# Reordering the first two column blocks of a gated up-projection on one core

## The chip, the cores and the metric

The kernel runs on one core of a Trainium2 chip. The number that counts is the device time of one execution, in microseconds (us). An execution runs five engines side by side, each with an instruction queue of its own that is worked off in order: PE (TensorE, matrix products; its weight loads are shown apart as PEld), DVE (VectorE), ACT (ScalarE), POOL (GpSimd) and SP (SyncE, which here issues the transfers). Engines wait for each other by semaphores.

## The reference

One layer of a transformer: 1024 positions, model width 1024, everything in float32.

```
h  = RMSNorm(x);  P = h @ W_in
A  = multi-head latent attention (MLA), 8 heads        -> 512 columns
Bm = chunked attention ("ca"), 8 heads                 -> 512 columns
x += concat(RMSNorm(A), RMSNorm(Bm)) @ W_out
u  = causal depthwise conv3( RMSNorm(x) @ W_up ) + conv_b      # W_up: 1024 x 5632, two halves g and v
x += ( silu(g) * v ) @ W_down                                  # W_down: 2816 x 1024
```

## The kernel before

**Products.** TensorE multiplies rounded operands. A float32 matrix is split into a rounded high part (a copy, on ACT) and a low part (value minus high part, a subtraction on DVE or POOL), and `mm3` makes one product of three matmuls: high by high, low by high, high by low (lines 137, 138 and 139 of the helper, so all products of the kernel carry these three lines). Here the high part is ready first and the low part one or two instructions later.

**Out-projection.** It goes by 8 tiles of 128 positions, in `order = [0, 4, 1, 5, 2, 3, 6, 7]`. The half that belongs to "ca" has been accumulated and added to x earlier; the last stage adds the half that belongs to "mla". Step i of that stage, for tile t = order[i], multiplies (`out_proj`), transposes the normalised rows of the tile before (`trans2`, line 1223), adds the product to x on DVE (`out_add`, line 1126), takes the norm (`norm2`), turns the tile before into its share of the operands of the next stage (`quarters`), and normalises its own rows on DVE (`scale2`, tile h, line 1173).

**Up-projection.** It goes by 22 column blocks j. The activations are cut into four quarters B11, B21, B22 and so on by positions and model width, the weights of a block into A11, A12, A21, A22, and a block is made of seven products instead of eight: A11, S2, S1, S3, A12, A22, S4 (12 matmuls each), with sums of weights (S1 to S4, on POOL) on one side and sums of activations (T1 to T4, held with high and low parts in tiles hq) on the other. `quarters` makes T1, T2, T3 of a tile with t >= 4 on DVE out of PSUM, their high parts on ACT and their low parts on POOL (`put(..., G)`, line 1209), and subtracts for T4 on POOL (line 1248). `make_w` and `put_w` split the weights (tiles wop, lines 1320 and 1325). `combine(j, n)` adds a finished product to the sums of its block: U2, U4, U3 and, in place, in the two double-bank PSUM tiles "ps" of the block (line 1404); one such tile is the "v" half of a block (S3 in one bank, A22 in the other), the second the "g" half (A12 and S4). Single banks are "pb". `conv` runs the three taps (ACT line 1349, DVE lines 1352 and 1353), `glu` the activation, and `pair` makes the four additions "as" on every odd block (DVE lines 1387 to 1390) for the down-projection.

**What sets the order.** The program is written out by hand; the order of the text is the order on each engine, there is no scheduler. `slot(d, fn)` puts a function d products later: `step()` counts the products of the loop over j, so `slot(1, ...)` runs after the next product has been issued. Block 0 and the first two products of block 1 are written out ahead of that loop, mixed with what belongs to the last tile (tile 7: `scale2(7)`, `trans2(7)`, its T1, T2, T3, B22). `make_early` splits the weights A11 and A12 of block 0 (tiles woph on ACT, wopl on POOL, lines 1259 and 1260); at the end of step i = 4 their transfer is issued.

A wait on PSUM is kept for a whole tile: a matmul into one bank of a "ps" tile waits for what reads or writes the other bank of it, where that stands ahead of it in the program.

Of the kernel before, what the change touches and what calls it, by code (L numbers as in the profile page):

```python
# [14 lines left out]
ALU = mybir.AluOpType  # L15
# [24 lines left out]
W0_LO_V = (1, "A11"), (1, "A12"), (0, "S4")  # L40
W_LO_V = "S2", "S1", "A22"
WO_AT = 146, 154, 162, 170
# [36 lines left out]
def trunk(ctx, tc, a, out):  # L79
# [4 lines left out]
    V, A, G, T = nc.vector, nc.scalar, nc.gpsimd, nc.tensor  # L84
# [17 lines left out]
    def blk(dt=F32, n="b"):  # L102
        return pool.tile([128, 1024], dt, name=name(n), tag="blk", bufs=NBLK)
# [4 lines left out]
    def small(tag, dt, n, bufs):  # L108
        return pool.tile([128, 512], dt, name=name(n), tag=tag, bufs=bufs)

    def p2(dt, n):
        return small("p2", dt, n, 10)
# [4 lines left out]
    def ps():  # L117
        return pp[0].tile([128, 1024], F32, name=name("ps"), tag="d", bufs=nb[0])

    def bank():  # L120
        return pp[0].tile([128, 512], F32, name=name("pb"), tag="b", bufs=nb[1])
# [11 lines left out]
    def f(ap):  # L133
        return ap.bitcast(F32)

    def mm3(o, lh, ll, rh, rl, start, stop):
        T.matmul(o, lh, rh, start=start, stop=False)  # L137
        T.matmul(o, lh, rl, start=False, stop=False)  # L138
        T.matmul(o, ll, rh, start=False, stop=stop)  # L139
# [366 lines left out]
    ca = {}  # L506
# [284 lines left out]
    slot = -8  # L791
# [240 lines left out]
    order = [0, 4, 1, 5, 2, 3, 6, 7]  # L1032
# [2 lines left out]

    def out_part(kind, t, c, j):
        if j == 0:
            if kind == "ca":
                part[kind, t, c] = bank()
            elif c == 0:  # L1040
                p = ps()
                part[kind, t, 0], part[kind, t, 1] = p[:, 0:512], p[:, 512:1024]
        wh, wl_ = wo[(4 if kind == "ca" else 0) + j]
        hi, lo = O[kind, j]
        w = slice(512 * c, 512 * c + 512)
        mm3(part[kind, t, c], hi[:, t * 128:(t + 1) * 128], lo[:, t * 128:(t + 1) * 128], wh[:, w], wl_[:, w], j == 0,
            j == 3)
# [29 lines left out]
    for s in range(NS + LAG):  # L1077
        if s < NS:
            n, i, pc_ = flat[s]
# [37 lines left out]
    def rows(d, t):  # L1117
        return d[t * 128:(t + 1) * 128]
# [82 lines left out]
    def put(name_, o, src, lo_eng, now=True):  # L1201

        s3 = src.rearrange("p (k s) -> p k s", k=4)
        for hi, ks in Q[name_].cols(0, o):
            A.activation(hi, s3[:, ks], AF.Copy)

        def lo_part():
            for (hi, ks), (lo, _) in zip(Q[name_].cols(0, o), Q[name_].cols(1, o)):
                lo_eng.tensor_tensor(lo, s3[:, ks], f(hi), op=ALU.subtract)  # L1209

        if now:
            lo_part()
        return lo_part
# [12 lines left out]
    def quarters(t, p):  # L1226
        u, o = t % 4, (t % 4) * 128
        if t == 3:
            F.append(blk(F32, "F"))
        F0 = F[u]  # L1230
        if t < 4:
            for i, n in enumerate(("B11", "B21")):
                lo = put(n, o, p[i], V, False)
                A.activation(F0[:, 512 * i:512 * i + 512], p[i], AF.Copy)
                lo()
            return
        T3, T1, T2 = [p2(F32, "T") for _ in range(3)]
        lo = put("B22", o, p[1], V, False)
        V.tensor_tensor(T1, p[0], F0[:, 0:512], op=ALU.subtract)
        A.activation(T3, p[0], AF.Copy)  # L1240
        lo()
        V.tensor_tensor(T2, p[1], T1, op=ALU.subtract)
        V.tensor_tensor(T3, p[1], T3, op=ALU.subtract)
        put("T1", o, T1, G)
        put("T2", o, T2, G)
        put("T3", o, T3, G)
        T4f[u] = T2
        G.tensor_tensor(T2, T2, F0[:, 512:1024], op=ALU.subtract)

    Q["B11"], Q["B21"] = Quarter(True), Quarter(True)  # L1250
# [11 lines left out]

    new_psum("psc", 2, 4)
    for i, t in enumerate(order):
        if i == 7:
            make_early()
        p = out_proj("mla", t, i == 7)
        q = trans2(order[i - 1]) if i else None
        out_add("mla", t, 0, p[0])
        out_add("mla", t, 1, p[1])  # L1270
        norm2(t)
        if i:
            quarters(order[i - 1], q)
        if i < 7:
            scale2(t)
            nc.sync.dma_start(rows(x2d, t), x2[t])
        if i < 6:
            load_x2(order[i + 2], x2d)
        if i == 4:
            for k in range(2):  # L1280
                nc.sync.dma_start(wst[k].rearrange("p (k c) -> p k c", k=4),
                                  dap(w_up, 4 * k * 128 * 2 * DFF, [[2 * DFF, 128], [128 * 2 * DFF, 4], [1, 128]]))

    ad = nc.dram_tensor("act_scratch", (7, NFF // 2, 128, 512), F32, kind="Internal").ap()
    wbig = big(F32, "wstage")
    NAMES = ("A11", "S2", "S1", "S3", "A12", "A22", "S4")
    HALF = {"A11": "B11", "A12": "B21", "S4": "B22", "A22": "T4", "S1": "T1", "S2": "T2", "S3": "T3"}

# [10 lines left out]
    def make_w(j, n, lag=1):  # L1299

        st = wbig[:, 2048 * (j % 2):2048 * (j % 2) + 2048]
        A11, A12, A21, A22 = [st[:, 512 * i:512 * i + 512] for i in range(4)]
        if n == "S2":
            S1 = wtmp["S1"] = p2(F32, "S1")
            S2 = wtmp["S2"] = p2(F32, "S2")
            G.tensor_tensor(S1, A21, A22, op=ALU.add)
            G.tensor_tensor(S2, S1, A11, op=ALU.subtract)
        if n == "S3":
            wtmp["S3"] = p2(F32, "S3")
            G.tensor_tensor(wtmp["S3"], A11, A21, op=ALU.subtract)  # L1310
        if n == "S4":
            wtmp["S4"] = p2(F32, "S4")
            G.tensor_tensor(wtmp["S4"], A12, wtmp["S2"], op=ALU.subtract)
        put_w(j, n, wtmp[n] if n in wtmp else {"A11": A11, "A12": A12, "A22": A22}[n], lag)
# [14 lines left out]
    pair = {}  # L1329
# [32 lines left out]
    def slot(d, fn):  # L1362

        if d:
            todo.setdefault(now[0] + d, []).append(fn)
        else:
            fn()
# [6 lines left out]
    def glu(j, g, v):  # L1374
        A.activation(g, g, AF.Silu)
        act[j] = v
        q = j // 2

        def mul():
            (V if j == NFF - 1 else G).tensor_tensor(v, g, v, op=ALU.mult)  # L1380
            slot(STORE, lambda: nc.sync.dma_start(ad[4 * (j % 2), q], v[:, 0:512]))

        def pair():
            e = act.pop(j - 1)
            A11, A21, A12, A22 = e[:, 0:512], e[:, 512:1024], v[:, 0:512], v[:, 512:1024]
            s = [p2(F32, "as") for _ in range(4)]
            V.tensor_tensor(s[0], A21, A22, op=ALU.add)  # L1387
            V.tensor_tensor(s[1], s[0], A11, op=ALU.subtract)  # L1388
            V.tensor_tensor(s[2], A11, A21, op=ALU.subtract)  # L1389
            V.tensor_tensor(s[3], A12, s[1], op=ALU.subtract)  # L1390

            def store():
                nc.sync.dma_start(ad[5, q], A22)
                for i, d in enumerate((2, 1, 3, 6)):
                    nc.sync.dma_start(ad[d, q], s[i])

            slot(STORE, store)

        slot(1, mul)
        if j % 2:  # L1400
            slot(2, pair)

    def add(d, x_, y, op=ALU.add):
        V.tensor_tensor(d, x_, y, op=op)  # L1404
# [54 lines left out]
    W21, W22 = wbig[:, 1024:1536], wbig[:, 1536:2048]  # L1459
    scale2(7)  # L1460
    make_w(1, "A11", 0)
    make_w(1, "A12", 0)
    S1 = p2(F32, "S1")
    V.tensor_tensor(S1, W21, W22, op=ALU.add)
    q = trans2(7)
# [3 lines left out]
    T3, T1, T2 = [p2(F32, "T") for _ in range(3)]  # L1469
    F0 = F[3]  # L1470
    V.tensor_tensor(T1, q[0], F0[:, 0:512], op=ALU.subtract)
    A.activation(T3, q[0], AF.Copy)  # L1472
    combine(0, "A11")
    V.tensor_tensor(T2, q[1], T1, op=ALU.subtract)
    V.tensor_tensor(T3, q[1], T3, op=ALU.subtract)
    put("T1", 384, T1, V)
    put_w(0, "S1", S1)
    product(0, "S1")
    lo = put("B22", 384, q[1], V, False)
    put("T2", 384, T2, V)  # L1480
    V.tensor_tensor(W21, wst[0], W21, op=ALU.subtract)
    V.tensor_tensor(wst[0], S1, wst[0], op=ALU.subtract)
# [2 lines left out]
    G.tensor_tensor(T2, T2, F0[:, 512:1024], op=ALU.subtract)  # L1485
    T4f[3] = T2
    product(0, "S2")
    lo()
    V.tensor_tensor(wst[1], wst[1], wst[0], op=ALU.subtract)
    put_w(0, "S4", wst[1])  # L1490
    product(0, "S4")
    put_w(0, "S3", W21)
    combine(0, "A12")
    product(0, "S3")
    Q["T4"] = Quarter(True)
    for u in range(4):
# [114 lines left out]
    for j in range(1, NFF):  # L1611
        for i, n in enumerate(NAMES):
            if j > 1 or n not in ("A11", "A12"):
                product(j, n)
            if j == NFF - 1:
                if i == 1:
                    ring += [big(F32R, "aring"), big(F32R, "wring")]
                if i < AHEAD:
                    load_step(*dsteps[i])
                if i >= 4:  # L1620
                    split_step(i - 4, *dsteps[i - 4])
            step()
            if i == 1 and j + 2 < NFF:
                load_up(j + 2)
            if j > 1 or n not in ("A11", "A12"):
                slot(1, lambda j=j, n=n: combine(j, n))
            if j + 1 < NFF:
                make_w(j + 1, n)
    xb += [big(F32, "x2b") for _ in range(2)]
    for n, (i, q) in enumerate(dsteps):  # L1630
# [8 lines left out]
        if n in X2_AT:  # L1639
            t = X2_AT.index(n)  # L1640
# [30 lines left out]
```

## Time and profile before

| | |
|---|---|
| time, median of 3 runs | 1291.77 us (1290.53 to 1293.58) |
| profiled execution: its own time | 1291.74 us |
| profiled execution: span in the trace | 1289.7 us |
| granted clock of TensorE, mean (1.0 is 2.4 GHz) | 0.991 |
| PE busy | 1230.5 us, 95% of the span |
| DVE busy | 968.5 us, 75% |
| POOL busy | 724.8 us, 56% |
| ACT busy | 634.0 us, 49% |

The span runs from the first to the last recorded instruction; the time of the execution is 2.0 us longer. All instants below are in us from the start of the span. The up-projection of the blocks spoken of here lies between 630 and 710.

### The profile page before, as it was taken

How to read it: one execution, taken by the hardware profiler on the slowest of the kernel's cores; microseconds unless marked ns; L12 is line 12 of the kernel's file. 1: busy time of each engine (PE TensorE's matmuls, PEld its weight loads, DVE VectorE, ACT ScalarE, POOL GpSimd, SP SyncE). 2: the span in 40 equal slices, each digit the busy share in tenths (PEclk: the TensorE clock that was granted, in tenths of full speed). 3: DMA queues.
4: the chain of work that ended last, by engine and by line, in shares of the span. 5: the costliest groups of instructions: out<-in, count | busy, mean ns of one | idle time of the engine just before them, and what ended most of it. 6: DMA issues, size and time to landing. Idle time of an engine off the chain costs nothing.

```text
span 1289.7 us, 17903 instructions
## 1 busy us (share of the span) xinstructions
PE 1230.5 (95%) x5920; PEld 1012.2 (78%) x5920; DVE 968.5 (75%) x1663; ACT 634.0 (49%) x1306; POOL 724.8 (56%) x753
## 2 busy tenths in 40 slices
PE   7999998999998988999979999999999999999998
PEld 7888886777786766788757888888888888878887
DVE  4786757888989898465886766776766777788983
ACT  6681344667776766404553443343343344434442
POOL 3578743667676777203675766766766750435630
PEclk9999999999999999999998999999999999999999
DMA  5101222111111121263513233233233236933253
GB/s 205 48 27 49 59 68 71 26 42 43 30 28 40 42 63 50 98 229 138 173 58 113 68 99 122 93 112 123 72 92 123 90 131 229 392 109 102 73 188 131
DMA packets 101315, 130.57 MB, mean 101 GB/s; under 512 B 11783, under 2 KB 60519, under 8 KB 101223
## 3 DMA queue, kind: packets, MB, share of 16 engines
q1 hardware_dynamic: 99431, 125.17, 29.8%
q0 software_dynamic: 1792, 4.26, 1.7%
q8 instruction: 47, 0.77, 0.2%
q14 instruction: 45, 0.37, 0.1%
HBM read 93.27 MB, written 31.81 MB: 97 GB/s over the span
## 4 chain that ended last, share of the span: by engine, by line
PE 50%; DVE 8%; issue 2%; ACT 1%; DMA 1%; POOL 0%; DVEq 0%; ACTq 0%; SPq 0%
PE pb L138 10%; PE pb L137 10%; PE pb L139 10%; PE ps L137 6%; PE ps L139 6%; PE ps L138 5%; DVE as L1388 1%; DVE ps L1404 1%; DVE as L1387 1%; DVE x2b L1404 1%; DVE as L1389 1%; DVE wop L1325 1%; DVE as L1390 0%; PE pb L1223 0%; DVE h L1173 0%
## 5 line engine op out<-in xcount | busy, mean ns | idle before, releaser
L921 POOL TENSOR_TENSOR plo<-misc,phi 128x512 fp32r<-128x512 f32 (+2 forms) x144 | 149.3, 1044 | 72.9 <-ACT phi L906 59.1
L137 PE MATMUL ps<-hq,wop 128*128 128x512 f32 x344 | 136.7, 397 | 9.9 <-DVE ps L1404 7.3
L1349 ACT ACTIVATE u<-ps,cols 128x1024 f32<-128x1024 f32 x44 | 53.1, 1207 | 187.0 <-DVE ps L1404 187.0
L139 PE MATMUL ps<-hq,wop 128*128 128x512 f32 x344 | 135.2, 393 | 1.2 <-DVE wop L1325 1.2
L138 PE MATMUL ps<-hq,wop 128*128 128x512 f32 x344 | 135.4, 393 | 0.2 <-DVE hq L1209 0.2
L903 ACT ACTIVATE misc<-pb 128x512 f32<-128x512 f32 (+1 forms) x192 | 89.3, 465 | 82.6 <-POOL plo L921 26.7
L1325 POOL TENSOR_TENSOR wop<-S,wop 128x512 fp32r<-128x512 f32 x42 | 62.7, 1492 | 108.0 <-ACT wop L1320 108.0
L138 PE MATMUL pb<-wring,aring 128*128 128x512 f32 x308 | 120.2, 390 | 1.9 <-DVE wring L1578 1.9
L137 PE MATMUL pb<-wring,aring 128*128 128x512 f32 x308 | 120.1, 390 | 0.1
L139 PE MATMUL pb<-wring,aring 128*128 128x512 f32 x308 | 120.0, 390 | 0.0
L137 PE MATMUL pb<-hq,wop 128*128 128x512 f32 x264 | 103.1, 391 | 2.0 <-ACT T L1472 1.0
L139 PE MATMUL pb<-hq,wop 128*128 128x512 f32 x264 | 103.0, 390 | 0.0
L138 PE MATMUL pb<-hq,wop 128*128 128x512 f32 x264 | 102.9, 390 | 0.0
L1575 DVE TENSOR_TENSOR aring<-ast,aring 128x512 fp32r<-128x512 f32 x77 | 71.2, 924 | 36.6 <-ACT aring L1574 36.6
L1574 ACT ACTIVATE aring<-ast 128x512 fp32r<-128x512 f32 x77 | 48.5, 630 | 95.1 <-PE pb L138 74.9
L137 PEld LDWEIGHTS ps<-hq,wop 128*128 128x128 f32 x344 | 65.3, 190 | 28.2 <-DVE ps L1404 13.0
L906 ACT ACTIVATE phi<-pb 128x512 fp32r<-128x512 f32 (+3 forms) x185 | 87.0, 470 | 0.0
L139 PEld LDWEIGHTS ps<-hq,wop 128*128 128x128 f32 x344 | 65.3, 190 | 15.3 <-DVE wop L1325 1.5
L138 PEld LDWEIGHTS ps<-hq,wop 128*128 128x128 f32 x344 | 65.4, 190 | 13.9 <-DVE hq L1209 0.7
L137 PE MATMUL pb<-wh,hTh 128*128 128x512 f32 x192 | 76.2, 397 | 0.0
L138 PE MATMUL pb<-wl,hTh 128*128 128x512 f32 x192 | 76.0, 396 | 0.1
L139 PE MATMUL pb<-wh,hTl 128*128 128x512 f32 x192 | 75.4, 393 | 0.0
(341 smaller groups left out, 3601.2 us busy)
## 6 DMA issues: line engine op xcount, KB each, us to landing
wstage<-in_w_up_dram SPq DMA_DIRECT2D x43, 512.0 KB
ast<-act_scratch SPq DMA_DIRECT2D x77, 256.0 KB
act_scratch<-as SPq DMA_DIRECT2D x44, 256.0 KB
wd<-in_w_down_dram SPq DMA_DIRECT2D x44, 256.0 KB
act_scratch<-u SPq DMA_DIRECT2D x33, 256.0 KB
x<-in_x_dram SPq DMA_DIRECT2D x16, 512.0 KB
ws<-in_w_in_dram SPq DMA_DIRECT2D x32, 256.0 KB
x_scratch<-x SPq DMA_DIRECT2D x14, 512.0 KB
```

Of the source, the lines that this page charges most:

```text
L137: T.matmul(o, lh, rh, start=start, stop=False)
L138: T.matmul(o, lh, rl, start=False, stop=False)
L139: T.matmul(o, ll, rh, start=False, stop=stop)
L903: A.activation(p32[:, w], o[:, w], AF.Exp, scale=sc_)
L906: A.activation(phi[:, w], o[:, w], AF.Exp, scale=sc_)
L921: e.tensor_tensor(plo[:, w], p32[:, w], f(phi[:, w]), op=ALU.subtract)
L1325: (V if n in W_LO_V or (j, n) in W0_LO_V else G).tensor_tensor(lo, s, f(hi), op=ALU.subtract)
L1349: A.activation(u, U, AF.Identity, scale=convw(2, c), bias=convb(c))
L1387: V.tensor_tensor(s[0], A21, A22, op=ALU.add)
L1404: V.tensor_tensor(d, x_, y, op=op)
L1574: A.activation(ah, s, AF.Copy)
L1575: V.tensor_tensor(al, s, f(ah), op=ALU.subtract)
```

## The change

Nothing is computed otherwise; what changes is the order of the program and, for a few operations, the engine or the kind of PSUM tile:

- (a) `out_part`: the first MLA tile (t == order[0]) is accumulated in two single banks rather than in a double-bank tile.
- (b) `quarters` of tile 6 (called in step i = 7): the low parts of its T1 and T2 are put off, and made on DVE instead of POOL, after `make_w(1, "A11", 0)`; its subtraction for T4 on POOL is put off to the same place.
- (c) `make_early` is called in step 6 rather than in step 7.
- (d) the four "as" additions of blocks 0 and 1 stand at slot 4 rather than at slot 2.
- (e) `combine(0, "A11")`, a copy on ACT, stands before `trans2(7)`.
- (f) the low part of the B22 quarter of tile 7 is made right after its high part, and both ahead of T1's parts.
- (g) `combine(0, "A12")` stands after `product(0, "S2")`, two products earlier.
- (h) `combine(1, "S3")` stands at slot 2 rather than at slot 1, that is after product A22 of block 1 has been issued.

```diff
     def out_part(kind, t, c, j):
         if j == 0:
-            if kind == "ca":
+            if kind == "ca" or t == order[0]:
                 part[kind, t, c] = bank()
...
-        put("T1", o, T1, G)
-        put("T2", o, T2, G)
+        late = [put("T1", o, T1, V if t == 6 else G, t != 6), put("T2", o, T2, V if t == 6 else G, t != 6)]
         put("T3", o, T3, G)
         T4f[u] = T2
+        if t == 6:
+            return late + [lambda: G.tensor_tensor(T2, T2, F0[:, 512:1024], op=ALU.subtract)]
         G.tensor_tensor(T2, T2, F0[:, 512:1024], op=ALU.subtract)
...
     for i, t in enumerate(order):
-        if i == 7:
+        if i == 6:
             make_early()
...
         if i:
-            quarters(order[i - 1], q)
+            late = quarters(order[i - 1], q)
...
         slot(1, mul)
         if j % 2:
-            slot(2, pair)
+            slot(2 if j > 1 else 4, pair)
...
     scale2(7)
     make_w(1, "A11", 0)
+    for fn in late:
+        fn()
     make_w(1, "A12", 0)
+    combine(0, "A11")
...
     A.activation(T3, q[0], AF.Copy)
-    combine(0, "A11")
     V.tensor_tensor(T2, q[1], T1, op=ALU.subtract)
     V.tensor_tensor(T3, q[1], T3, op=ALU.subtract)
+    put("B22", 384, q[1], V)
     put("T1", 384, T1, V)
     put_w(0, "S1", S1)
     product(0, "S1")
-    lo = put("B22", 384, q[1], V, False)
     put("T2", 384, T2, V)
...
     product(0, "S2")
-    lo()
+    combine(0, "A12")
     V.tensor_tensor(wst[1], wst[1], wst[0], op=ALU.subtract)
     put_w(0, "S4", wst[1])
     product(0, "S4")
     put_w(0, "S3", W21)
-    combine(0, "A12")
     product(0, "S3")
...
             if j > 1 or n not in ("A11", "A12"):
-                slot(1, lambda j=j, n=n: combine(j, n))
+                slot(2 if (j, n) == (1, "S3") else 1, lambda j=j, n=n: combine(j, n))
```

Line numbers behind the first hunks move by one, and by three or four from the sixth hunk on (1404 becomes 1405, 1387 becomes 1388, 1325 becomes 1326, 1471 becomes 1475).

On PE, where product A22 of block 1 begins and S4 follows (ps_7324 and ps_7325 are the "v" tile of block 1, ps_7367 and ps_7368 its "g" tile), the rows of before are:

```order
L139 MATMUL ps_7324<-hq_6562,wop_7263 128x512
L137 MATMUL ps_7324<-hq_7215,wop_7266 128x512 [waits DVE_49]
L138 MATMUL ps_7324<-hq_7215,wop_7266 128x512
...
L139 MATMUL ps_7324<-hq_7215,wop_7266 128x512
L137 MATMUL ps_7367<-hq_6549,wop_7289 128x512 [waits Activation_49]
```

and of the change, on the same engine at the same place:

```order
L139 MATMUL ps_7325<-hq_6562,wop_7264 128x512
L137 MATMUL ps_7325<-hq_7216,wop_7267 128x512
L138 MATMUL ps_7325<-hq_7216,wop_7267 128x512
...
L139 MATMUL ps_7325<-hq_7216,wop_7267 128x512
L137 MATMUL ps_7368<-hq_6549,wop_7290 128x512 [waits DVE_49,Activation_49]
```

The first matmul of A22 waited for DVE and no longer waits; the first matmul of S4, twelve rows later, has a wait for DVE beside the one for ACT (it belongs to the taps of block 0, which read the "g" tile of block 0).

On DVE, between `scale2(7)` and the operations on tile 7 (S is the weight sum S1 of block 0, T the sums T1, T2, T3, hq their parts; 7023 and 7024 belong to tile 6), the rows of before are:

```order
L1173 SCALAR_TENSOR_TENSOR h_7015<-x_6915,stat,gffn_6248 128x512 x2
L1325 TENSOR_TENSOR wop_7079<-wstage_7045,wop_7079 128x512
L1325 TENSOR_TENSOR wop_7082<-wstage_7045,wop_7082 128x512
L1464 TENSOR_TENSOR S_7085<-wstage_7045 128x512
L1471 TENSOR_TENSOR T_7124<-pb_7087,F_6960 128x512
L1474 TENSOR_TENSOR T_7125<-pb_7092,T_7124 128x512
L1475 TENSOR_TENSOR T_7123<-pb_7092,T_7123 128x512
L1209 TENSOR_TENSOR hq_6555<-T_7124,hq_6553 128x2x128
```

and of the change:

```order
L1173 SCALAR_TENSOR_TENSOR h_7016<-x_6916,stat,gffn_6248 128x512 x2
L1326 TENSOR_TENSOR wop_7075<-wstage_7041,wop_7075 128x512
L1209 TENSOR_TENSOR hq_6555<-T_7023,hq_6553 128x2x128
L1209 TENSOR_TENSOR hq_6556<-T_7023,hq_6554 128x2x128
L1209 TENSOR_TENSOR hq_6559<-T_7024,hq_6557 128x2x128
L1209 TENSOR_TENSOR hq_6560<-T_7024,hq_6558 128x2x128
L1326 TENSOR_TENSOR wop_7083<-wstage_7041,wop_7083 128x512
L1468 TENSOR_TENSOR S_7088<-wstage_7041 128x512
L1475 TENSOR_TENSOR T_7127<-pb_7090,F_6969 128x512
L1477 TENSOR_TENSOR T_7128<-pb_7095,T_7127 128x512
L1478 TENSOR_TENSOR T_7126<-pb_7095,T_7126 128x512
L1209 TENSOR_TENSOR hq_6551<-pb_7095,hq_6549 128x2x128
```

Four low parts of tile 6, which stood on POOL, are now on DVE ahead of the T1 of tile 7, and the low part of B22 stands ahead of that of T1.

On DVE in block 2 (U_7451, U_7470 and U_7491 are its sums, ps_7455 its "v" tile, ps_7476 its "g" tile, as the additions on the activations of blocks 0 and 1), the rows of before are:

```order
L1404 TENSOR_TENSOR ps_7455<-ps_7455,U_7470 128x512
L1387 TENSOR_TENSOR as_7508<-u_7294,u_7400 128x512
L1388 TENSOR_TENSOR as_7509<-as_7508,u_7294 128x512
L1389 TENSOR_TENSOR as_7510<-u_7294 128x512
L1390 TENSOR_TENSOR as_7511<-u_7400,as_7509 128x512
L1404 TENSOR_TENSOR ps_7476<-ps_7476,P_7425 128x512
L1404 TENSOR_TENSOR ps_7455<-U_7491,ps_7455 128x512
```

and of the change:

```order
L1405 TENSOR_TENSOR ps_7456<-ps_7456,U_7471 128x512
L1405 TENSOR_TENSOR ps_7477<-ps_7477,P_7426 128x512
L1405 TENSOR_TENSOR ps_7456<-U_7492,ps_7456 128x512
L1388 TENSOR_TENSOR as_7545<-u_7295,u_7401 128x512
L1389 TENSOR_TENSOR as_7546<-as_7545,u_7295 128x512
```

The combinations of A12 and of A22 of block 2 now stand ahead of the four additions.

## Rows read from the trace of the kernel before

**Rows 1.** The page: span, and part 1 (busy us, share, instructions).

```profile
span 1289.7 us, 17903 instructions
...
PE 1230.5 (95%) x5920; PEld 1012.2 (78%) x5920; DVE 968.5 (75%) x1663; ACT 634.0 (49%) x1306; POOL 724.8 (56%) x753
```

**Rows 2.** Timeline of PE, start of MLA: start, us, instruction, count, [idle before <-releaser].

```profile
578.09 0.39 PE L139 MATMUL pb<-woh,oca 128*128 128x512 f32 x1
579.32 0.50 PE L137 MATMUL ps<-wom,oh 128*128 128x512 f32 x1 [0.84 <-DVE x L1126]
```

**Rows 3.** Timeline of PE, blocks 0 to 2.

```profile
642.51 0.50 PE L137 MATMUL pb<-hq,wop 128*128 128x512 f32 x1 [1.00 <-ACT T L1472]
...
649.26 0.47 PE L137 MATMUL pb<-hq,wop 128*128 128x512 f32 x1 [0.97 <-DVE hq L1209]
...
659.83 0.50 PE L139 MATMUL ps<-hq,wop 128*128 128x512 f32 x1 [1.18 <-DVE wop L1325]
...
669.36 0.47 PE L137 MATMUL ps<-hq,wop 128*128 128x512 f32 x1 [1.48 <-ACT wop L1320]
...
677.72 0.79 PE L137 MATMUL ps<-hq,wop 128*128 128x512 f32 x1 [5.38 <-DVE ps L1404]
...
686.13 0.39 PE L137 MATMUL pb<-hq,wop 128*128 128x512 f32 x1
...
704.50 0.51 PE L137 MATMUL ps<-hq,wop 128*128 128x512 f32 x1 [1.89 <-DVE ps L1404]
```

**Rows 4.** Windows: stretch, us, busy PE, PEld, DVE, ACT, POOL, clock, DMA, GB/s.

```profile
677.70:684.00 6.30, 6.28 (x15) 4.97 (x16) 0.75 (x2) 0.02 (x1) 1.12 (x1) 0.52 0.29 83
```

**Rows 5.** Timeline of DVE, A22 of block 1 and its surroundings.

```profile
667.93 1.28 DVE L1353 SCALAR_TENSOR_TENSOR u<-ps,cols,u 128x1022 f32<-128x1022 f32 x1
...
676.99 0.68 DVE L1404 TENSOR_TENSOR ps<-ps,U 128x512 f32<-128x512 f32 x1
683.25 0.70 DVE L1404 TENSOR_TENSOR ps<-U,ps 128x512 f32<-128x512 f32 x1 [5.58 <-PE ps L139]
```

**Rows 6.** Timeline of DVE, block 2: the four additions and what follows.

```profile
698.41 1.43 DVE L1387 TENSOR_TENSOR as<-u,u 128x512 f32<-128x512 f32 x1
...
703.76 0.69 DVE L1404 TENSOR_TENSOR ps<-ps,P 128x512 f32<-128x512 f32 x1
```

**Rows 7.** Timeline of DVE beside POOL, last tiles and block 0.

```profile
621.26 1.40 DVE L1173 SCALAR_TENSOR_TENSOR h<-x,stat,gffn 128x512 f32<-128x512 f32 x2
...
627.65 3.47 DVE L1173 SCALAR_TENSOR_TENSOR h<-x,stat,gffn 128x512 f32<-128x512 f32 x2
...
641.09 0.68 DVE L1471 TENSOR_TENSOR T<-pb,F 128x512 f32<-128x512 f32 x1
...
643.29 0.76 DVE L1209 TENSOR_TENSOR hq<-T,hq 128x256 fp32r<-128x256 f32 x2
...
655.61 2.49 DVE L1209 TENSOR_TENSOR hq<-T,hq 128x512 fp32r<-128x512 f32 x4
658.02 1.75 DVE L1325 TENSOR_TENSOR wop<-wstage,wop 128x512 fp32r<-128x512 f32 x1
```

**Rows 8.** Timeline of POOL in the same stretch.

```profile
627.60 2.97 POOL L1260 TENSOR_TENSOR wopl<-wst,woph 128x512 fp32r<-128x512 f32 x2 [1.36 <-ACT woph L1259]
634.62 6.01 POOL L1209 TENSOR_TENSOR hq<-T,hq 128x256 fp32r<-128x256 f32 x6 [0.24 <-ACT hq L1205]
...
648.11 1.62 POOL L1209 TENSOR_TENSOR hq<-T,hq 128x256 fp32r<-128x256 f32 x2 [5.80 <-ACT hq L1205]
```

**Rows 9.** Timeline of PE, the transposes that wait for h.

```profile
629.59 0.63 PE L1223 MATMUL pb<-identr,h 128*128 128x128 f32 x4 [0.40 <-DVE h L1173]
631.27 0.63 PE L1223 MATMUL pb<-identr,h 128*128 128x128 f32 x4 [1.05 <-DVE h L1173]
```

**Rows 10.** Timeline of ACT, what `make_early` follows: now, and a tile earlier.

```profile
620.01 0.60 ACT L1234 ACTIVATE F<-pb 128x512 f32<-128x512 f32 x1
...
626.40 0.60 ACT L1234 ACTIVATE F<-pb 128x512 f32<-128x512 f32 x1
```

## The prediction

> **What bounds the kernel now.** I read the page first, then the waits of PE, then the timeline of PE over the edited stretch, and then DVE and POOL beside it. The page [rows 1] has PE busy for 95% of the span, DVE for 75%, POOL for 56%: only time that PE stands still, or runs at a lower clock, can be won. So the reader should look for PE's gaps inside the edited stretch, about 579 to 710 us, and ask of each which instruction ends it.
>
> There are seven such gaps worth naming [rows 2, 3], and two at the transposes [rows 9]. The longest is 5.38 us, at 677.72, ahead of the first matmul of A22 of block 1; it is put down to a combination on DVE, and the DVE timeline [rows 5] has that combination at 676.99, ending at 677.67, just before PE goes on. The stretch behind it is at a granted clock of 0.52 [rows 4], the lower of the two levels (1.2 GHz): 15 matmuls fill 6.28 us there. The next gap, 1.89 us at 704.50, ends with a combination on DVE at 703.76 [rows 6] that stood behind the four additions, which occupy DVE from 698.41 on.
>
> A product of 12 matmuls takes 2.72 to 2.75 us: from 686.13 to 704.50 there are six products and the gap of 1.89 [rows 3], (18.37 - 1.89) / 6.
>
> **(a) Single banks for the first MLA tile.** The gap of 0.84 at 579.32 [rows 2] is a wait for DVE reading the last "ca" tile, and a first MLA matmul into a double-bank tile needs a whole tile free. With single banks it waits for an older reader, done some ten us earlier. From 578.09 one matmul pitch of 0.23 would lead to 578.32; it started at 579.32. The gain is 1.0. What hides it afterwards: nothing; the next tile has had no gap of this kind. Bounds: 0 to -1.0.
>
> **(h) combine(1, "S3") behind A22.** In the order A22 of block 1 loses its wait altogether, and S4 of block 1 gets one for the taps of block 0. So 5.38 goes, and with it the half clock: A22 and S4 of block 1 took 686.13 - 677.72 = 8.41 where two products take 5.50, so 2.91 more. Together 8.29 us. The next wait in line is the taps: their second pass begins 667.93 and the last of four (1.28 each) ends about 671.7 [rows 5], while S4 begins one product after A22. If A22 starts at S3's end (669.36 + 2.75 = 672.1), S4 starts at 674.9; the taps leave 3 us of room. Behind it the last combination of block 1 still has a full product of cover.
>
> **(d) The additions two products later.** PE's gap of 1.89 and 0.15 of slow first matmuls go: -2.05. The additions, 5.35 us of DVE [rows 6], then stand ahead of the last combination of block 2 and the taps; PE needs these two "ps" tiles back in S3 and A12 of block 3. By my working there are 0.6 to 0.9 us of room there, and at A22 of block 3 between 0 and 1.3 us of new gap. I take 0, and 1.3 for the range.
>
> **(c) Earlier weights.** In step 7 DVE's two operations h took 3.47 us, beside 2.97 us of wopl on POOL [rows 7, 8], where a tile earlier, alone, they took 1.40 [rows 7]: they ran in turns, 1.03 more for each operation met. That gave PE's gaps of 0.40 and 1.05 at the transposes [rows 9], 1.8 us with the slow matmuls behind them. A tile earlier the ACT operation that the weights follow ends at the same distance from h: 620.01 against 621.26 for h, now 626.40 against 627.65 [rows 7, 10]. So the same meeting happens one tile earlier. I take 0. Bounds: -1.8 if it misses h, +0.5 if the later start of the tile behind is not given back.
>
> **(b), (e), (f): the work on tile 7.** Four low parts come to DVE ahead of T1 of tile 7; two of such width take 0.76 [rows 7], so 1.5 us. POOL loses four of the six low parts that took 6.01 [rows 8], so the operations of DVE around them (h, wop) meet fewer. I take T1 1.2 later: 642.3 where it was 641.09 [rows 7]. The copy of A11's product now stands ahead of the T copy on ACT, so A12 of block 1 follows A11 at once: its gap of 1.00 at 642.51 [rows 3] goes. But nothing is won by that, since product S1 behind it needs T1, whose parts are 1.2 later, and the 0.76 of B22's low part [rows 7] is ahead of them too: the gap is moved to before S1 and grows. Worked through operation by operation, S1 starts at 646.3 and ends at 649.6, where it ended at about 648.2 (649.26 less the gap of 0.97 [rows 3]): +1.4. S2 loses its wait of 0.97 for B22, gets a short one for T2, and ends at 653.0 against 652.0: +1.0. S4's weights, behind more on DVE, make it end 1.6 later.
>
> **(g), and the T4 parts behind it.** Moving combine(0, "A12") lets DVE start the four T4 low parts and the low weights of A22 at about 654.1. In before they stood behind that combination, at 655.61 and 658.02 [rows 7]. The rows have 2.49 for four and 1.75 for the weights, which met a POOL operation. POOL's sums of block 1 (three S operations and a low part) would now be met by all: five operations without meeting are 2.49 + 0.72 = 3.2, four meetings at 1.03 are 4.1, so 7.3, and the weights come at 661.4. PE's third matmul of A22 of block 0 then starts at 661.47 against 659.83 [rows 3]: +1.6. By the row of before alone, 2.49 + 1.75 = 4.24, they come at 658.3, ahead of the end of S3 at 659.15, and there is no gap at all: 2.3 less than I take. The Trainium skill ("SBUF — State Buffer", section "SBUF: two separate sides") says that a DVE operation with two SBUF inputs and a GpSimd operation that reads SBUF exclude each other for the whole instruction; by that rule nothing on DVE is gained by an earlier start while POOL has work, which is the dearer sum. The trace agrees in the h rows (3.47 against 1.40).
>
> From there +1.6 is carried on: S2 and S1 of block 1 follow without gap, S3 needs the first taps of block 0, which are 1.6 later with A22, so the gap of 1.48 at 669.36 [rows 3] stays and S3 starts at 670.95. Three products of 2.72 follow without a wait (S3, A22, S4: 673.7, 676.4, 679.1), so block 2 begins at 679.1 where it began at 686.13 [rows 3]: -7.0. That is the 8.29 of (h) plus 0.3 of slow first matmuls, less 1.6 of lateness.
>
> **Sum.** -1.0 (a) - 7.0 (blocks 0 and 1) - 2.05 (d) = -10.05. The profiled execution took 1291.74 (span 1289.7 and 2.0 around it), which is the median of 1291.77 within 0.03. So 1281.7.
>
> **The rivals.**
>
> Fewer meetings. If DVE's operations meet POOL's less than I count, the extra 1.3 of lateness goes, the 2.3 at A22 of block 0 and the 1.48 at S3 shrink too. With no meeting at all in the new places I get block 2 at 673, 6 us earlier: 1275.4. Half of it gives 1278.5. For it: POOL's gaps (5.80 before its low parts at 648.11 [rows 8]) leave DVE alone often. Against: the rows of h.
>
> The clock falls elsewhere. Two of the remaining gaps are 2.3 to 2.4 us long (ahead of S1 and at A22 of block 0); before, only the gap of 5.38 had the half clock behind it in this stretch, those up to 1.89 had not [rows 3, 4]. Half clock cost 2.91 behind that gap. If one fall of about that length came, it is partly hidden, since PE then waits less for DVE later: 1.7 each. With the 1.3 at block 3 this gives 1283.4 with one, 1286.4 with two and that gap.
>
> The change does not do what it says. If A22's wait was only the last to end, and S4's new wait for the taps, or the tile's other users, hold PE as long, 5.38 comes back one product later with the half clock: -1.0 - 2.05 + 0 to 1.5 gives 1288.7 to 1290.2. Against: the taps end 3 us too early for it.
>
> The other side: DVE becomes the bound in block 0. From h of tile 7 to the A22 weights I count 24 operations with two SBUF inputs on DVE; in the sum 12 of them meet POOL. If the others do as well, 12 x 1.03 = 12.4 us more, 1294.1. It decides from ten on (10.05 / 1.03). Against: POOL had idle 5.80 just there [rows 8] and loses four operations, so it hasn't the work to meet them with.
>
> **How the numbers follow.** The forecast has 0.60, fewer meetings 0.13, clock falls or the gap at block 3 0.17, the change that doesn't act 0.06, the other side 0.04. About 0.2% (2.6 us) is what a measurement of this kernel can tell from no change, so faster means under 1289.2. The first three are faster: 0.90; half of the fourth too: 0.93; the other half is within: 0.04 with a little of the fifth; slower 0.03. The range takes the forecast, the nearer half of fewer meetings (from 1277.5) and the clock falls up to 1286.0; it leaves out some 0.06 + 0.02 + 0.10.
>
> **What would show it.** Right: no gap at the first MLA matmul; no wait at A22 of block 1 and the full clock through blocks 1 and 2; the gap ahead of the last product of block 2 gone; T1 about 1 us later; a gap of some 2.3 at A22 of block 0; h drawn out to about 3.5 one tile earlier. Wrong: a fall of the clock behind the gaps ahead of S1 or at A22 of block 0; a wait at S4 of block 1 or in block 3; DVE busy without a pause from 636 to 662.

## The result, and the profile after

| | before | changed |
|---|---|---|
| time, median | 1291.15 us (1289.54 to 1293.58, 4 runs) | 1282.24 us (1280.23 to 1283.94, 4 runs) |
| profiled execution: span, TensorE's mean clock | 1289.7 us, 0.991 | 1281.7 us, 0.993 |

The ratio is 0.9937, with a 95% interval of 0.9917 to 0.9957: faster by 0.6%. The time lies within the predicted range, 0.5 us from the predicted 1281.7. The first lines of the page of the changed kernel:

```profile
span 1281.7 us, 17905 instructions
## 1 busy us (share of the span) xinstructions
PE 1228.4 (96%) x5920; PEld 1010.8 (79%) x5920; DVE 973.3 (76%) x1667; ACT 634.7 (50%) x1306; POOL 721.9 (56%) x749
```

PE's own work is what it was [rows 1]; the time went out of its pauses. The timeline of PE of the changed kernel, at the places of [rows 2, 3, 9]:

```profile
578.74 0.39 PE L139 MATMUL pb<-woh,oca 128*128 128x512 f32 x1
578.97 0.39 PE L137 MATMUL pb<-wom,oh 128*128 128x512 f32 x1
...
622.74 0.63 PE L1223 MATMUL pb<-identr,h 128*128 128x128 f32 x4 [0.35 <-DVE h L1173]
624.41 0.63 PE L1223 MATMUL pb<-identr,h 128*128 128x128 f32 x4 [1.05 <-DVE h L1173]
...
645.82 0.50 PE L137 MATMUL pb<-hq,wop 128*128 128x512 f32 x1 [2.27 <-ACT wop L1321]
...
661.13 0.50 PE L139 MATMUL ps<-hq,wop 128*128 128x512 f32 x1 [1.18 <-DVE wop L1326]
...
670.66 0.47 PE L137 MATMUL ps<-hq,wop 128*128 128x512 f32 x1 [1.53 <-ACT wop L1321]
...
673.47 0.39 PE L137 MATMUL ps<-hq,wop 128*128 128x512 f32 x1
...
678.91 0.39 PE L137 MATMUL pb<-hq,wop 128*128 128x512 f32 x1
...
695.23 0.39 PE L137 MATMUL ps<-hq,wop 128*128 128x512 f32 x1
...
697.95 0.39 PE L137 MATMUL pb<-hq,wop 128*128 128x512 f32 x1
...
712.57 0.50 PE L137 MATMUL ps<-hq,wop 128*128 128x512 f32 x1 [0.85 <-DVE ps L1405]
```

The gaps at the first MLA matmul (578.97), at A22 of block 1 (673.47) and at the last product of block 2 (695.23) are gone. The gap ahead of S1 has grown to 2.27, the two at the transposes stand one tile earlier, and one of 0.85 is new, at A22 of block 3 (712.57).

The windows of the changed kernel, with the columns of [rows 4]: the stretch behind the gap of 2.27, and A22 and S4 of block 1.

```profile
646.70:650.20 3.50, 3.45 (x9) 2.67 (x10) 2.77 (x6) 1.24 (x3) 0.46 (x1) 0.54 0.00 0
673.40:679.00 5.60, 5.60 (x27) 4.63 (x26) 5.60 (x6) 1.64 (x4) 5.60 (x4) 1.00 0.14 50
```

The clock now falls to the lower level, 1.2 GHz, behind the gap of 2.27 (0.54), and A22 and S4 of block 1 run at the full one.

DVE and POOL of the changed kernel, where the T4 parts are made (the timeline of DVE first, then that of POOL):

```profile
620.80 3.47 DVE L1173 SCALAR_TENSOR_TENSOR h<-x,stat,gffn 128x512 f32<-128x512 f32 x2
...
641.79 0.68 DVE L1475 TENSOR_TENSOR T<-pb,F 128x512 f32<-128x512 f32 x1
...
653.61 5.78 DVE L1209 TENSOR_TENSOR hq<-T,hq 128x512 fp32r<-128x512 f32 x4
659.32 1.76 DVE L1326 TENSOR_TENSOR wop<-wstage,wop 128x512 fp32r<-128x512 f32 x1
```

```profile
654.81 1.74 POOL L1307 TENSOR_TENSOR S<-wstage 128x512 f32<-128x512 f32 x1
656.63 1.61 POOL L1308 TENSOR_TENSOR S<-S,wstage 128x512 f32<-128x512 f32 x1
658.87 1.65 POOL L1311 TENSOR_TENSOR S<-wstage 128x512 f32<-128x512 f32 x1 [0.63 <-DVE hq L1209]
```

The four T4 low parts begin 2.0 earlier than in [rows 7] and take 5.78 where they took 2.49, in turns with POOL's weight sums; the A22 weights begin at 659.32, where it was 658.02.

**A clock for the comparison.** From one profiled execution to the next, the part ahead of the edits and the part behind them vary. Over the fourteen executions profiled, the last "ca" matmul starts at 573.5 to 581.1 us, and from block 4 to the last matmul it takes 558.0 to 562.0 us. So the versions are also compared by the start of a product on PE less the start of the last "ca" matmul (before: 578.09 [rows 2]; changed: 578.74). Block 2 then starts at 686.13 - 578.09 = 108.04 before and at 678.91 - 578.74 = 100.17 in the changed kernel.

| version (its label below) | block 2 starts | block 3 | block 4 | median, us | ratio to before, 95% interval |
|---|---|---|---|---|---|
| before | 108.04 | 129.31 | 148.35 | | |
| changed | 100.17 | 119.21 | 139.40 | 1282.24 | 0.9937 (0.9917 to 0.9957) |
| changed, once more (e11) | 100.15 | 119.19 | 139.40 | 1282.05 | 0.9933 (0.9916 to 0.9951) |
| changed without (h) (e1) | 108.41 | 127.45 | 146.52 | 1289.30 | 0.9992 (0.9980 to 1.0003) |
| before with (h) (e2) | 99.61 | 124.06 | 143.12 | 1287.52 | 0.9971 (0.9955 to 0.9986) |
| before with (a), (d), (h) (e3) | 98.47 | 117.51 | 137.95 | 1282.79 | 0.9942 (0.9923 to 0.9960) |
| changed without (d) (e4) | 100.23 | 125.45 | 144.91 | 1287.98 | 0.9978 (0.9967 to 0.9989) |
| changed, wopl on DVE (e5) | 98.36 | 117.40 | 137.86 | 1281.31 | 0.9933 (0.9921 to 0.9945) |
| changed without (b) (e6) | 98.97 | 118.01 | 137.10 | 1282.26 | 0.9933 (0.9916 to 0.9950) |
| changed without (g) (e8) | 100.59 | 119.63 | 138.73 | 1283.22 | 0.9944 (0.9931 to 0.9957) |
| e3, wopl on DVE, (h) in block 3 too (e9) | 96.67 | 115.71 | 137.04 | 1281.47 | 0.9932 (0.9920 to 0.9944) |
| e3, wopl on DVE (e7) | 96.62 | 115.66 | 136.10 | 1281.97 | 0.9924 (0.9906 to 0.9941) |
| e7 with the additions at slot 10 (e10) | 96.62 | 115.66 | 134.70 | 1279.51 | 0.9914 (0.9899 to 0.9929) |
| changed without (b), wopl on DVE (e12) | 97.23 | 116.27 | 135.31 | 1277.24 | 0.9889 (0.9872 to 0.9907) |

Over 578 to block 4 the changed kernel wins 148.35 - 139.40 = 8.95 us, which is the measured gain within its interval. The instants repeat: in a second profile of the changed kernel they are within 0.02. The runs of versions whose medians are 1 to 3 us apart overlap, and where the medians and the instants say different things, that is said below. The instants end at block 4, and not all of a lead there lasts. From block 4 to the start of the down-projection all fourteen take 346.5 to 346.8 us; but in the down-projection the four versions built on e3 (e3, e7, e9, e10) have a wait of PE for DVE (tile x2b) of 1.5 to 2.1 us, where the other ten have 0.5 or less. Why, no run shows.

### The profile page after: what moved, and what is told of

Same layout as the page of the kernel before. It is cut to its first block, busy times and chain, and to the rows that moved or that the text cites. A ratio compares the mean times of both kernels' runs of the same rounds, so it can differ in the third digit from the quotient of the medians.

```text
span 1281.7 us, 17905 instructions
## 1 busy us (share of the span) xinstructions
PE 1228.4 (96%) x5920; PEld 1010.8 (79%) x5920; DVE 973.3 (76%) x1667; ACT 634.7 (50%) x1306; POOL 721.9 (56%) x749
## 4 chain that ended last, share of the span: by engine, by line
PE 47%; DVE 8%; issue 2%; POOL 1%; ACT 1%; DMA 1%; SPq 0%; DVEq 0%; POOLq 0%; ACTq 0%
PE pb L139 10%; PE pb L137 10%; PE pb L138 10%; PE ps L137 5%; PE ps L139 5%; PE ps L138 5%; DVE as L1389 1%; DVE ps L1405 1%; DVE as L1391 1%; DVE as L1388 1%; DVE x2b L1405 0%; DVE h L1173 0%; DMA ast<-act_scratch 0%; DVE as L1390 0%; DVE aring L1577 0%
## 5 line engine op out<-in xcount | busy, mean ns | idle before, releaser
L137 PE MATMUL ps<-hq,wop 128*128 128x512 f32 x344 | 135.0, 393 | 3.5 <-ACT wop L1321 1.5
L139 PE MATMUL ps<-hq,wop 128*128 128x512 f32 x344 | 134.1, 390 | 1.2 <-DVE wop L1326 1.2
L138 PE MATMUL ps<-hq,wop 128*128 128x512 f32 x344 | 134.0, 390 | 0.1
```

## The experiments

**Without (h), and (h) alone.**

```diff
-                slot(2 if (j, n) == (1, "S3") else 1, lambda j=j, n=n: combine(j, n))
+                slot(1, lambda j=j, n=n: combine(j, n))
```

> The changed kernel with edit (h) undone: the combination of S3 of block 1 stands again one product after it, ahead of A22. Theory (the gap at A22 and the half clock behind it are what the change wins): the combination ends at about 679.1 in the changed kernel, so A22 of block 1 waits 5.6 us where it waits 0 and starts at about 679.2 instead of 673.5, with the half clock behind it (2.9 us): 8.3 us later in all, about 1290.5 us. Rival (the other edits in blocks 0 and 1 take the work off VectorE that made it late, and (h) only renames the wait): less than 2 us later, 1282 to 1284.

Measured: 0.9992 of before, 7.12 us later at block 4 than the changed kernel. PE's timeline at A22 of block 1 of this version, and its window:

```profile
678.47 0.79 PE L137 MATMUL ps<-hq,wop 128*128 128x512 f32 x1 [5.41 <-DVE ps L1405]
```

```profile
678.40:684.70 6.30, 6.23 (x16) 4.90 (x17) 0.73 (x3) 0.00 (x0) 1.17 (x1) 0.57 0.28 83
```

The wait and the half clock are back, 108.41 - 100.17 = 8.24 at block 2, as the theory had it (8.3); 1.12 of it is regained at block 3's A22, whose gap this version doesn't have. Without (h) the interval of the ratio holds 1; the instants leave 148.35 - 146.52 = 1.83 us of the gain.

The same line put the other way round into the kernel before:

> The kernel before with edit (h) alone. Theory: S3 of block 1 starts at 669.4 as before, A22 follows without a wait at 672.1, block 2 begins at 677.6 instead of 686.1: 8.3 to 8.5 us less than before, about 1283, and the gap of 1.9 ahead of the last product of block 2 stays. Rival (without the edits of block 0 VectorE is too late, the wait moves to S4 or to the next block): at most 3 us less, 1288 or more.

Measured: 0.9971, a median of 1287.52, between the theory's 1283 and the rival's 1288. At block 2 the theory is met: 99.61, 8.43 less than before. But then PE runs into the next wait (its timeline, and the window behind it):

```profile
696.57 0.79 PE L137 MATMUL ps<-hq,wop 128*128 128x512 f32 x1 [3.73 <-DVE ps L1404]
```

```profile
696.50:699.50 3.00, 2.93 (x7) 2.35 (x8) 1.21 (x3) 1.72 (x2) 0.55 (x1) 0.50 0.93 279
```

The gap ahead of the last product of block 2, 1.89 in [rows 3], is 3.73 here, with the lower clock behind it. So the theory's gap of 1.9 did not stay what it was; of 8.43 us, 5.25 are left at block 3.

**Without (d).**

```diff
-            slot(2 if j > 1 else 4, pair)
+            slot(2, pair)
```

> The changed kernel with (d) undone: the four additions stand again at slot 2. Theory: the gap of about 1.9 us ahead of S4 of block 2 comes back (2.05 with the slow matmuls behind it) and the gap of 0.9 in block 3 goes: 1.2 us more than the changed kernel, 1283.4. Rival (the additions fall into time that VectorE has free now that block 2 begins 7 us earlier): no gap at S4 of block 2, 0 to 0.8 us less.

Measured: 0.9978, and 5.51 us later at block 4 than the changed kernel, far beyond the 1.2. The same gap is 3.45 us (PE's timeline), and the timeline of DVE ahead of it shows why it is not 1.9:

```profile
696.30 0.80 PE L137 MATMUL ps<-hq,wop 128*128 128x512 f32 x1 [3.45 <-DVE ps L1405]
```

```profile
689.90 1.76 DVE L1388 TENSOR_TENSOR as<-u,u 128x512 f32<-128x512 f32 x1 [1.09 <-POOL u L1381]
691.70 1.67 DVE L1389 TENSOR_TENSOR as<-as,u 128x512 f32<-128x512 f32 x1
693.29 1.75 DVE L1390 TENSOR_TENSOR as<-u 128x512 f32<-128x512 f32 x1
694.96 0.68 DVE L1391 TENSOR_TENSOR as<-u,as 128x512 f32<-128x512 f32 x1
```

The additions need the product of the activation on POOL (u, line 1381). With block 2 starting 8 us earlier, DVE comes to them before POOL has it and stands 1.09, with the two combinations behind it in its queue. So (d) is worth 5.5 once (h) is in; to the kernel before it would be worth some 2.05, an estimate from [rows 3], as no run has (d) alone. The rival, that the additions find room by themselves, is out.

**Only (a), (d) and (h).** The three edits put into the kernel before, without (b), (c), (e), (f), (g).

> The kernel before with (a), (d) and (h), without (b), (c), (e), (f) and (g). Theory (b, c, e, f, g only bring work to VectorE ahead of block 1, and cost the lateness of 1.3 us that the changed kernel has at S3 of block 1): 1.0 + 8.4 + 2.05 less 0.8 at block 3, 10.6 us less than before, 1280.6, that is 1 to 1.7 us less than the changed kernel. Rival (those edits pay for themselves by the waits of 1.0 and 1.0 that they take away in block 0): 1 to 2 us more than the changed kernel, 1283 to 1284.

Measured: 148.35 - 137.95 = 10.40 less than before at block 4 against 8.95 for the changed kernel, so the instants bear out the theory by 1.45 us; the medians (0.9942 beside 0.9937, in different sessions) do not show it. In the profiled executions the lead is gone at the end: from block 4 to the last matmul this version takes 562.0 us and the changed kernel 559.1, and the wait named above, 1.93 here with the lower clock behind it and 0.46 there, is a large part of that.

**Without (b).** The low parts of T1 and T2 of tile 6 go back to POOL:

```diff
-        late = [put("T1", o, T1, V if t == 6 else G, t != 6), put("T2", o, T2, V if t == 6 else G, t != 6)]
+        put("T1", o, T1, G)
+        put("T2", o, T2, G)
...
-    for fn in late:
-        fn()
...
```

> The changed kernel with (b) undone: the low parts of T1 and T2 of tile 6 and its T4 subtraction are on GpSimd again and in the old place. Theory (the four low parts on VectorE ahead of T1 are what makes S1 late): T1 of tile 7 starts about 1 us earlier, the gap of 2.3 us ahead of S1 shrinks to about 1.2 and has no half clock behind it; of this 0.5 to 1.2 us reaches block 2: 1281 to 1281.7. Rival (GpSimd's six low parts beside h and the weights cost VectorE as much as the four low parts do): T1 starts when it does now, no difference within 0.3 us.

Measured: PE's gap ahead of S1 is 0.87, there is no half clock behind it, and block 2 starts 1.20 earlier (98.97). The theory, at its upper end. Block 4 is 2.30 earlier, since the gap at A22 of block 3 is absent too (the rows that tell why stand under "Block 3" below). The median, 1282.26, shows none of it; the six runs of this version spread from 1276.92 to 1285.27.

**Without (g).**

```diff
     product(0, "S2")
-    combine(0, "A12")
...
     put_w(0, "S3", W21)
+    combine(0, "A12")
     product(0, "S3")
```

> The changed kernel with (g) undone: combine(0, A12) stands again ahead of product S3, behind S4. Theory (the T4 low parts that (g) lets start earlier only take turns with GpSimd's weight sums, 5.8 us for four instead of 2.5): the T4 parts start 2 to 3 us later, take about 2.5 us, and the A22 weights come within 0.5 us of where they come now: no difference within 0.5 us, 1282.2. Rival (the early start is worth its 2 us): A22 of block 0 waits 2 us longer, 1284.

Measured: block 2 starts 0.42 later (100.59). The timeline of DVE of this version:

```profile
654.70 0.70 DVE L1405 TENSOR_TENSOR ps<-ps,P 128x512 f32<-128x512 f32 x1 [2.66 <-PE ps L139]
655.31 2.86 DVE L1209 TENSOR_TENSOR hq<-T,hq 128x512 fp32r<-128x512 f32 x4
658.10 1.76 DVE L1326 TENSOR_TENSOR wop<-wstage,wop 128x512 fp32r<-128x512 f32 x1
```

DVE waits 2.66 for S4 and then takes 2.86 for the four T4 parts instead of 5.78: while it waits, POOL does its sums alone. The theory holds: of the earlier start that (g) gives, 0.4 us arrive at block 2; at block 4 the version without (g) is even 0.67 ahead, as it lacks the gap at A22 of block 3.

**The early weights on DVE.** In the changed kernel, the two subtractions for wopl are made by VectorE behind the x additions of step 6:

```diff
-            G.tensor_tensor(lo, wst[k], f(hi), op=ALU.subtract)
             wop[0, n] = hi, lo
+
+    def early_lo():
+        for k, n in enumerate(("A11", "A12")):
+            V.tensor_tensor(wop[0, n][1], wst[k], f(wop[0, n][0]), op=ALU.subtract)
...
         out_add("mla", t, 1, p[1])
+        if i == 6:
+            early_lo()
```

> The changed kernel with the two wopl low parts of make_early on VectorE behind the x additions of step 6, instead of on GpSimd beside h. Theory (h takes 3.47 us only because it takes turns with wopl): h takes 1.4 us there, both gaps at the transposes (0.35 and 1.05) go, and the two low parts (1.4 us) fit VectorE's pause of 1.76 us: 1.8 us less than the changed kernel, 1280.4. Rival (h is late for reasons of its own, or the pause doesn't hold the low parts): the gaps stay or move one step on, 0 to 1.4 us more.

Measured: block 2 starts 1.81 earlier (98.36). DVE's timeline:

```profile
618.07 1.41 DVE L1173 SCALAR_TENSOR_TENSOR h<-x,stat,gffn 128x512 f32<-128x512 f32 x2
619.70 1.41 DVE L1126 SCALAR_TENSOR_TENSOR x<-ps,stat,x 128x512 f32<-128x512 f32 x2 [0.23 <-PE ps L139]
621.03 1.29 DVE L1265 TENSOR_TENSOR wopl<-wst,woph 128x512 fp32r<-128x512 f32 x2
```

The h that took 3.47 beside wopl takes 1.41, PE waits for it nowhere, and the two subtractions, 1.29 on DVE where POOL needed 2.97 [rows 8], fill a pause. At block 4, 1.54 of it is left, since the gap at A22 of block 3 is 1.12 here; the ratio, 0.9933 beside 0.9937, does not show it.

**Further versions.** The first is e3 with the early weights on DVE and, against the new gap, the combination of S3 behind A22 in block 3 as well:

> A version of its own: the kernel before with (a), (d) and (h) alone, the wopl low parts on VectorE behind the x additions of step 6, and the combination of S3 put behind A22 in block 3 too. Theory: 10.5 us less than before as (a), (d), (h) alone gave in the traces, 1.8 for the gaps at the transposes, 1.1 for the gap at A22 of block 3: 13.4 us less than before, about 1278.2. Rival (these gaps are kept up by the next wait in line): 1281 or more.

Measured: 0.9932, a median of 1281.47, where the rival has it; block 4 at 137.04, 11.31 less than before instead of 13.4. The gap at A22 of block 3 is gone, and another stands one product later, ahead of S4 of block 3 (PE's timeline, then DVE's):

```profile
710.36 0.50 PE L137 MATMUL ps<-hq,wop 128*128 128x512 f32 x1 [1.99 <-DVE ps L1409]
```

```profile
708.41 0.69 DVE L1409 TENSOR_TENSOR U<-ps,U 128x512 f32<-128x512 f32 x1 [2.95 <-PE ps L139]
709.02 0.69 DVE L1409 TENSOR_TENSOR ps<-ps,U 128x512 f32<-128x512 f32 x1
709.62 0.69 DVE L1409 TENSOR_TENSOR ps<-ps,P 128x512 f32<-128x512 f32 x1
```

DVE now waits 2.95 for A22, because the combination of S3 reads the tile that A22 writes; and behind it stands the combination of A12, in the double-bank tile that S4 writes next. In block 1 A12 has a single bank (`(j, n) != (1, "A12")` in `product`), so by the program there is no such wait behind (h) there, and in block 3 there is.

> The kernel before with (a), (d), (h) and the wopl low parts on VectorE, the combination of S3 in block 3 left in its old place. Theory (each gap taken away is won where no later wait takes it): block 2 starts at the same instant as in the version that also moved the combination of block 3, 11.4 us earlier than before, and the last product of block 3 has neither the gap of 2.0 nor the half clock that this move brought; the gap at A22 of block 3 is 0 or 1.1: 12.4 to 13.5 us less than before. Rival (the move in block 3 was not what brought the gap of 2.0): the gap stays, 11.3 less than before.

Measured: 0.9924; block 4 at 136.10, 12.25 less than before. The gap ahead of S4 is gone and that of 1.1 at A22 is back: the move was what brought the 2.0. The expectation's words on a half clock were wrong; there was none in that stretch of e9.

> The same with the four additions of blocks 0 and 1 at slot 10, ahead of the A22 combination of block 3, where VectorE waits 2.5 and 1.4 us for TensorE. Theory (the additions ahead of the taps of block 2 make VectorE late in block 3): the gap at A22 of block 3 is gone, 13.4 us less than before. Rival (they make the taps of block 3 late instead, 5.4 us of work against 3.9 us of pause): a new gap of 1 to 2 us in block 4, 11.5 to 12.5 less than before.

Measured: 0.9914; block 4 at 134.70, 13.65 less than before. A gap of 0.3 in block 4 is what is left in blocks 3 and 4: in this version the additions ahead of the taps of block 2 were what made DVE late.

> The changed kernel once more, beside the two versions on the same chip. Both theories: 8.9 us less than before from the first MLA matmul to block 4, with the gap of about 0.9 at A22 of block 3 if it belongs to the order of the program; without it, 9.8 less, if it hangs on how VectorE and GpSimd happen to meet in an execution.

Measured: 8.95 again, with the gap of 0.9 (0.86): it does not change from one execution of this program to the other.

> The changed kernel with (b) undone and the wopl low parts on VectorE. Theory (the two gains are of different stages and add up): 1.2 and 1.8 us less than the changed kernel at block 2, 0.9 more if the gap at A22 of block 3 is absent as it was with (b) undone: 3 to 3.9 less than the changed kernel. Rival (an earlier h only lets VectorE meet GpSimd's low parts sooner): 1.5 to 2 less.

Measured: the fastest of all, 0.9889 (0.9872 to 0.9907), 1277.24 against 1282.05 for the changed kernel on the same chip. Block 2 starts 2.94 earlier than in the changed kernel and block 4 4.09 earlier, a little more than the theory's 3 to 3.9; the gap at block 3 is absent. PE's waits from 560 to 760 in this version (for what; us in total, times, longest):

```profile
PE ps L139 <- DVE wop L1330: 1.8, 2, 1.2
PE ps L137 <- ACT wop L1325: 1.5, 1, 1.5
PE pb L137 <- ACT wop L1325: 0.9, 1, 0.9
...
```

The instants have e10 0.6 ahead of e12, the medians e12 ahead by 2.3; in the down-projection e10 has the wait of 1.5 and e12 one of 0.3. Between these two nothing is settled.

(c), (e) and (f) were not undone one by one; what they cost or give is known only together with (b) and (g), from e3.

## Why the prediction was right

- **(a)**, -1.0: the first MLA matmul is 0.23 behind the last "ca" matmul, one pitch, where it was 1.23. Exact, in each version that has (a).
- **Blocks 0 and 1**, -7.0: 108.04 - 100.17 = 7.87, less the 1.0 of (a): 6.87. That the gap at A22 and the clock behind it are its whole source is shown by e1 (8.24 back) and e2 (8.43 alone); no version has a gap at S4 of block 1, so the tap wait that S4 got is never the last to end. One reading was off, without effect on the sum: the wait of 1.48 at S3 is put down in the prediction to the taps of block 0, while its row has the high part of S3's weights on ACT (wop, line 1320). It stays as forecast, 1.53.
- **The lateness ahead of block 1**, +1.6: the third matmul of A22 of block 0, which waits for the low weights, starts at 661.13, 82.39 behind the "ca" matmul where it was 81.74; with the 1.0 of (a), 1.65 more. The meetings that it was counted from (five operations in 7.3 us) are in the rows: 653.61 to 661.08 is 7.47. The lower sum, with no meeting in the new place, did not come. That a meeting draws the operations out is shown by e5 and e8, where h takes 1.41 (e5) and the four T4 parts 2.86 (e8) with POOL's work elsewhere. The Trainium skill's rule ("SBUF — State Buffer", "SBUF: two separate sides") that a DVE operation with two SBUF inputs and a GpSimd operation that reads SBUF exclude each other for the whole instruction agrees with these runs. But the lateness does not go with that one meeting: in e8 the T4 parts begin only behind S4, and the matmul comes 0.4 later still. It comes with the edits (b), (c), (e), (f), (g), as e3, without them, has none of it, and 1.2 of it with (b) (e6).
- **(c)**, 0: the meeting moved by a tile, as said, with gaps of 0.35 and 1.05 where they were 0.40 and 1.05. Of the two bounds the -1.8 was open to whoever also moves wopl off POOL (e5).
- **(d)**, -2.05: from block 2 to block 3, 21.27 became 19.04, so 2.23. As a difference to before that is right. As the worth of the edit it is not: e4 puts it at 5.5, because the gap that (d) removes grows with (h), to 3.45 in e4 and 3.73 in e2, and the lower clock follows it. The sum could hide this, since both terms were taken from the trace of before, in which (h) was not yet made.
- **Block 3**, 0 taken, 1.3 as the bound: the gap of 0.85 came, 1.15 with the slow matmuls (20.19 where it was 19.04). This is the term that was mis-sized. The additions at slot 4 make it possible (e10, without them there, has no gap at A22), but they are not its whole cause: e1, e6, e8 and e12 have them at slot 4 and have no such gap. What differs is which goes first where the last addition meets a low part of weights on POOL. The rows of DVE and POOL in the changed kernel, then in e6:

```profile
698.01 1.80 DVE L1391 TENSOR_TENSOR as<-u,as 128x512 f32<-128x512 f32 x1
697.96 1.29 POOL L1326 TENSOR_TENSOR wop<-S,wop 128x512 fp32r<-128x512 f32 x1 [1.75 <-ACT wop L1321]
```

```profile
693.38 0.68 DVE L1390 TENSOR_TENSOR as<-u,as 128x512 f32<-128x512 f32 x1
693.37 1.83 POOL L1325 TENSOR_TENSOR wop<-S,wop 128x512 fp32r<-128x512 f32 x1 [1.83 <-ACT wop L1320]
```

In the first, POOL begins 0.05 ahead and DVE's addition takes 1.80; in the second both begin within 0.01, the addition takes 0.68 and POOL's operation 1.83. The 1.1 stays with DVE up to A22 of block 3. All nine traces with the additions at slot 4 that keep S3's combination of block 3 in its place are of one kind or the other: the addition takes 1.8 and the gap is there (changed, e3, e5, e7, e11), or it takes 0.7 and the gap is not (e1, e6, e8, e12).

- **The clock behind S1's gap**, a rival: it fell, as the rival said, and cost nothing that arrived at block 2, since PE then waited for the A22 weights on DVE anyway: in e5 the clock stayed up behind a gap of 2.24 at the same place, T1 was 1.78 earlier for want of the gaps at the transposes, and block 2 gained 1.81, no more. The price of 1.7 in that rival was too high by all of it.

Two of the signs that the prediction had named for being wrong came, this fall of the clock and the wait in block 3. The one cost nothing at block 2, and the other stayed inside its bound.

By its terms the forecast is 1.1 off: 0.2 more from (d), against 0.1 less from blocks 0 and 1 and 1.15 lost at block 3. That it is only 0.5 from the median is luck: the median of before, from which it was counted, was 1291.77 then and is 1291.15 with a fourth run, and this hides 0.6.

## What to carry to other kernels

Look at each gap of the bounding engine for the instruction that ends it, and then ask what stands behind that instruction in its queue. Here 7.1 of 8.95 us hang on one line that let a product go ahead of a combination (e1); alone it kept 5.2 of its 8.4 at block 4 (e2), and the rest came only with the four additions moved as well. Terms taken from one trace don't add up where one edit makes the engine arrive earlier at the place of the next. When an operation can be done by either of two engines, ask what it meets in its new place: the two subtractions of e5 fell into a pause of DVE and gave 1.8 us, while the four low parts that (b) brought to DVE cost 1.2 at block 2 (e6), and the earlier start that (g) gave was spent on meetings but for 0.4 (e8).

## What the runs showed of the hardware

The granted clock fell to the lower level behind the gap of 2.27 ahead of S1 in the changed kernel, and behind one of 2.21 in its second profile (e11), and not behind one of 2.24 at the same place in e5 (window of e5, columns of [rows 4]: the clock is 1.00):

```profile
641.00:646.00 5.00, 4.41 (x16) 2.75 (x17) 4.27 (x9) 2.09 (x6) 0.79 (x1) 1.00 0.02 5
```

In e5 PE had not had the pauses of 0.35 and 1.05 at the transposes some 20 us earlier; S2 began 4.9 us after S1 in the changed kernel and 3.6 in e5. The runs here don't tell whether those pauses or something else decided it. The length of the gap alone does not: behind the gap of 1.99 in e9 the clock stayed at the upper level, and at the wait in the down-projection it stayed up behind 2.14 in e9 and fell behind 1.93 in e3.

Where an operation of DVE and one of POOL met, a few hundredths of a microsecond decided which of them was drawn out: with POOL 0.05 ahead, a DVE addition took 1.80 us instead of 0.68 (changed kernel); with the two starts within 0.01, POOL's subtraction took 1.83 instead of 1.29 (e6).
